# Trunk kernel, layer 0: indexer products over all 128 rows with stacks one pair ahead, shorter top-k rounds, packed rotation, later statistics

## The chip, the cores and the metric

The kernel runs on one core of one Trainium2 chip. The metric is the device time of one execution in microseconds (us), lower is better. All matrix products are float32, most of them as three products of rounded high and low parts.

## The reference, cut to what matters

A two-layer trunk over 1024 tokens of width 1024. Only layer 0's first mixer is touched. Cut down, it is:

```python
proj = xn @ w_in
q, k, v, u, iq, iw, ik = jnp.split(proj, AB_SPLITS, axis=-1)
q = rope_partial(rmsnorm(q, q_gain), pos)    # 4 heads of 128, the first 32 rows turned
k = rope_partial(rmsnorm(k, k_gain), pos)
iq = rope_partial(iq, pos)                   # 16 index heads of 64
ik = rope_partial(ik, pos)                   # one index key of 64
s = jnp.einsum('bqhd,bsd->bqhs', iqb, ik)    # per block of 128 queries
scores = jnp.einsum('bqhs,bqh->bqs', jax.nn.relu(s), iwb)
scores = jnp.where(causal, scores, -jnp.inf)
_, idx = lax.top_k(scores, 256)              # 256 keys per query
p = softmax(q . k[idx] * scale); a = p @ v[idx]
b = multiscale_pool(u, pool_w) * pool_scale  # windows 2, 4, 8, 16
h = h + jnp.concatenate([a, b]) @ w_out
```

## The kernel before, in words

Arrays are held transposed, features on the 128 partitions and tokens along the free axis. A float32 matrix is split into a rounded part (hi) and a rest (lo), and one product is three TensorE instructions (`mm3`, lines 321 to 323). A scheduler orders the instructions of each engine ahead of time by the order of the program and its dependencies; `issue_after` keeps one TensorE instruction behind another.

**Indexer** (`mixer0`, lines 652 to 697). Sixteen index heads are worked off in eight pairs, m = 0 to 7. `iq_gemm(m)` (line 594) projects a pair to a 128-row tile: 24 matmuls of 512 columns and 24 of 256. At the head of pass m the tile is turned by position (lines 655 to 658: a shuffle on DVE, a product on POOL, a product and a sum on DVE) and made into two stacks of 128 rows, one per head: the head's hi rows in its own 64 partitions, its lo rows in the other 64 (ACT line 661, DVE line 662). Then for the query blocks i = 2 to 7 and both heads, the scores against nk = 128(i+1) keys are summed in PSUM from two products per 512 columns:

```python
nc.tensor.matmul(p[:, c:c + n], stk[j][:, q0:q0 + P], ikh[:, c:c + n], start=True, stop=False)
last = nc.tensor.matmul(p[:, c:c + n], stk[j][own, q0:q0 + P], ikl[own, c:c + n], start=False, stop=True)
```

The first (line 672) takes all 128 rows, the second (line 673) the 64 hi rows. ACT applies the ReLU out of PSUM (line 679, two PSUM buffers, seven SBUF ones), DVE adds the weighted result to the block's scores `sc[i]` (line 689, 687 for the first head). After each such step two steps (three matmuls each) of `iq_gemm(m + 2)` are put in, which last for 8 of the 12 steps of a pass with m < 6, and from m = 1 on one step of the first key head's product every fourth time.

**Search** (`top_k`, lines 719 to 790). The 256th largest score of each query is found bit by bit, for the blocks 5, 7, 6 together and then for 4, 3, 2: two passes of 16 rounds each, 64 rounds in all. In a round DVE counts, for two of the three blocks, the keys not below a candidate (line 738), ACT counts the third by a sum of signs (line 749, blocks 5 and 4), and four small DVE instructions on 128x3 make the next candidate (lines 752, 753, 755, 756).

**Projections** (lines 792 to 895), beside the search: four pool groups `u`, the key heads `k1` to `k3` and four query heads `q`, 48 matmuls of 512 columns each, in the order of `PROJ` (line 207), then 192 matmuls for v. For k and q `head_stats` (line 639) copies the product, squares it (ACT line 642), sums the squares with eight tiny matmuls into the one PSUM bank of tag B (line 348), and DVE and POOL make the inverse root (lines 339, 340; for q also line 342, copied at line 862). `rope` (lines 809 to 816) turns the first 32 rows of each head in two halves: shuffle and sum on DVE (813, 816), two products on POOL (814, 815). k is then scaled by its root (line 869), q goes to memory (line 863). The rest of an item (`out`) runs one item later.

**Attention** (lines 901 to 990) makes the bias from the found bound, and the softmax and its products for all four heads, first for blocks 5, 7, 6 between the rounds of the second search. Loads and stores stand on SP's queue in order; the weights come two blocks ahead, their hi parts made by ACT (line 105), their lo parts by POOL or DVE (line 106).

Of the kernel before, what the change touches and what calls it, by code (L numbers as in the profile page):

```python
# [19 lines left out]
P = 128  # L20
# [27 lines left out]
def trunk_kernel(ctx: ExitStack, tc: tile.TileContext, io, dbg=None):  # L48
# [158 lines left out]
    PROJ = ("u3", "k1", "u2", "q0", "u1", "k2", "u0", "q1", "k3", "q2", "q3")  # L207
# [327 lines left out]
    def mixer0(right):  # L535
# [94 lines left out]
        def key_gemm(hd):  # L630
            w = W.next()
            t = heads[hd] = A(name="k"), []
            for half in range(2):
                p = G(name="pqk")
                yield from gemm_steps(p, w, xn, half)
                head_stats(t[0], t[1], p, half, V_AK, None)
            yield

        def head_stats(t, rss, p, half, gain, post):
# [3 lines left out]
            ss = B(name="ss")  # L643
            token_sums(ss, sq, HALF)
            rss.append(rstd_of(ss[:, :4], 4, 1.0 / P, post=post))
# [5 lines left out]
        side, turns = side_steps(), 0  # L651
        for m in range(8):
# [3 lines left out]
            nc.gpsimd.tensor_tensor(iq, iq, ciq[:, 256:], op=ALU.mult)  # L656
            nc.vector.tensor_tensor(sh, sh, siq[:, 256:], op=ALU.mult)
            nc.vector.tensor_tensor(iq, iq, sh, op=ALU.add)
            stk = [A((P, QI), F32R, "stk") for _ in range(2)]
            for j, (own, other) in enumerate(((lo64, hi64), (hi64, lo64))):  # L660
                nc.scalar.activation(stk[j][own], iq[own], AF.Copy)
                nc.vector.tensor_tensor(stk[j][other], iq[own], stk[j][own].bitcast(F32), op=ALU.subtract)
            ahead = iq_gemm(m + 2) if m < 6 else iter(())
            next(ahead, None)
            for i in range(2, 8):
                nk = (i + 1) * P
                for j, own in enumerate((lo64, hi64)):
# [29 lines left out]
            run(ahead)  # L697
        run(side)
# [8 lines left out]
        ACT_COUNTS = (5, 4)  # L707
# [12 lines left out]
        def top_k(bt):  # L720
            n = len(bt)

            def col(dt, name):
                return cpool.tile([P, n], dt, name=nm(name))

            cnt, cand, ncand, base, ge, need, sgn, off = (col(F32, nme) for nme in (
                "cnt", "cand", "ncand", "base", "ge", "need", "sgn", "off"))
            bits, low = col(U32, "bits"), col(U32, "low")
            by_act = {b for b in range(n) if bt[b] in ACT_COUNTS}
            for b in range(n):  # L730
                nc.gpsimd.memset(need[:, b:b + 1], 2.0 * TOPK - (bt[b] + 1) * P if b in by_act else float(TOPK))
# [9 lines left out]
            def search():  # L741

                nc.vector.memset(base, 0.0)
                nc.vector.memset(cand, 32768.0)
                nc.vector.memset(ncand, 0.5 - 32768.0)
# [49 lines left out]
        cqk, sqk = (pp.tile([32, T], F32, name=n) for n in ("cqk", "sqk"))  # L795
        nc.sync.dma_start(cqk, io["rope_q"][0])
        nc.sync.dma_start(sqk, io["rope_q"][1])
# [4 lines left out]
        rsq = keyp.tile([P, 8, 4], F32, name="rsq")  # L802
# [3 lines left out]
        def ptile(name):  # L806
            return pp.tile([P, T], F32, tag="t", bufs=3, name=nm(name))

        def rope(t):
            for half in range(2):  # L810
                sh = H("xt")[:32]
                th = t[:32, hs(half)]
# [5 lines left out]
        kT, v, wins = [], [], []  # L818

        def pool_in(g):  # L820
# [24 lines left out]
            return out  # L845

        def head_in(which, hd):
            if hd in heads and not which:
                t, rss = heads[hd]
            else:  # L850
                w = W.next()
# [845 lines left out]
```

## Time and profile before

| | us |
|---|---|
| median of 3 runs (lowest to highest) | 3076.42 (3075.61 to 3080.59) |
| the profiled execution, device time | 3071.26 |
| its span | 3069.1 |
| PE busy | 2890.0 (94%) |
| DVE busy | 1962.0 (64%) |
| ACT busy | 1249.3 (41%) |
| POOL busy | 868.6 (28%) |

The span is what the hardware profiler saw between the first and the last instruction of the core. PE is TensorE, DVE VectorE, ACT ScalarE, POOL GpSimd, SP the queue of loads and stores. PE's instructions are pipelined, and their ends are modelled: the distance from one start to the next says more than a duration. PEclk is the granted TensorE clock, 1.00 for 2.4 GHz and 0.50 for 1.2 GHz; a mean between them is a mix in time. The stretch that the change touches goes from 113.9 us (first score product) to 722.4 us (first output product); after it the program is as it was.

### The profile page before, as it was taken

The numbers are of one execution on the slowest core, as the hardware profiler recorded it, in microseconds if no ns is written. First come the engines' busy times: TensorE is split into PE (matmuls) and PEld (weight loads), VectorE is DVE, ScalarE is ACT, GpSimd is POOL, SyncE is SP. The second block draws the span as 40 slices with busy tenths as digits, with TensorE's granted clock in tenths as the row PEclk, the third lists the DMA queues.
The fourth block names the chain that finished last, engine by engine and source line by source line (L and its number), as shares of the span: only waits on it lengthen the run. The fifth ranks groups of instructions, "written<-read, shape, count | busy, mean of one in ns | idle before, by whom it ended". The sixth has DMA issues, their size and how long they took to land. (4 is left out here: it accounts for less than half of the span.)

```text
span 3069.1 us, 36440 instructions
## 1 busy us (share of the span) xinstructions
PE 2890.0 (94%) x13022; PEld 2279.7 (74%) x13022; DVE 1962.0 (64%) x3092; ACT 1249.3 (41%) x2058; POOL 868.6 (28%) x661
## 2 busy tenths in 40 slices
PE   7999888899999989999999997999999999999999
PEld 6665566678888868887778765777788878777877
DVE  8666799985345584445775865666633554566876
ACT  6444333565354443333333314333545443322432
POOL 5311344221132154443330101001101344455332
PEclk9998788999999999999999998999999999999999
DMA  6200011324443424334535745775463334555544
GB/s 233 69 21 21 21 50 40 110 67 149 163 157 132 129 86 123 124 119 148 173 123 175 251 138 178 254 244 181 146 204 124 138 113 127 166 185 196 168 135 143
DMA packets 169637, 423.75 MB, mean 138 GB/s; under 512 B 19376, under 2 KB 33840, under 8 KB 169456
## 3 DMA queue, kind: packets, MB, share of 16 engines
q1 hardware_dynamic: 169456, 421.43, 42.0%
q8 instruction: 103, 1.69, 0.2%
q14 instruction: 78, 0.64, 0.1%
HBM read 323.18 MB, written 98.17 MB: 137 GB/s over the span
## 5 line engine op out<-in xcount | busy, mean ns | idle before, releaser
L105 ACT ACTIVATE w<-raw 128x512 fp32r<-128x512 f32 (+4 forms) x497 | 382.7, 786 | 615.5 <-POOL raw L169 126.8
L106 DVE TENSOR_TENSOR w<-raw,w 128x512 fp32r<-128x512 f32 (+3 forms) x438 | 417.0, 968 | 218.6 <-ACT w L105 216.8
L106 POOL TENSOR_TENSOR w<-raw,w 128x1024 fp32r<-128x1024 f32 (+1 forms) x59 | 145.6, 2470 | 365.3 <-ACT w L105 364.3
L167 POOL TENSOR_TENSOR acc<-raw 128x512 f32<-128x512 f32 (+1 forms) x64 | 85.0, 1329 | 410.6 <-DMA raw<-in_w_down 188.8
L106 DVE TENSOR_TENSOR w<-acc,w 128x512 fp32r<-128x512 f32 (+1 forms) x64 | 77.4, 1210 | 145.0 <-ACT w L105 144.9
L321 PE MATMUL pa<-T,w 128*128 128x512 f32 x352 | 139.9, 397 | 12.5 <-DVE sq L1236 9.0
L322 PE MATMUL pa<-T,w 128*128 128x512 f32 x352 | 138.9, 395 | 0.2 <-DVE T L106 0.2
L323 PE MATMUL pa<-T,w 128*128 128x512 f32 x352 | 138.6, 394 | 0.0
L738 DVE TENSOR_SCALAR_CACHE_REDUCE junk<-key,cand 128x896 uint16<-128x896 uint16 (+3 forms) x128 | 116.3, 942 | 1.9
L135 ACT ACTIVATE w<-raw 128x1024 fp32r<-128x1024 f32 (+1 forms) x72 | 68.0, 950 | 119.4 <-PE pa L323 26.5
L105 ACT ACTIVATE w<-acc 128x512 fp32r<-128x512 f32 (+1 forms) x64 | 38.9, 609 | 159.6 <-POOL acc L167 151.8
L749 ACT ACTIVATE sq<-key,ncand 128x768 bf16<-128x768 uint16 (+1 forms) x64 | 56.3, 880 | 115.3 <-DVE cand L756 106.5
L322 PE MATMUL pr<-o,w 128*128 128x512 f32 x256 | 101.6, 397 | 0.0
L321 PE MATMUL pq<-hn,w 128*128 128x512 f32 x256 | 101.0, 395 | 0.0
L322 PE MATMUL pq<-hn,w 128*128 128x512 f32 x256 | 100.1, 391 | 0.0
L323 PE MATMUL pr<-o,w 128*128 128x512 f32 x256 | 99.9, 392 | 0.0
L323 PE MATMUL pq<-hn,w 128*128 128x512 f32 x256 | 99.7, 389 | 0.0
L689 DVE SCALAR_TENSOR_TENSOR sc<-relu,iw,sc 128x640 f32<-128x640 f32 (+3 forms) x60 | 73.0, 1220 | 41.1 <-ACT relu L679 40.4
L321 PE MATMUL pr<-o,w 128*128 128x512 f32 x256 | 98.1, 397 | 0.7 <-DVE ha L1119 0.5
L361 DVE TENSOR_TENSOR acc<-acc,sq 128x512 f32<-128x512 f32 (+1 forms) x105 | 86.9, 829 | 17.3 <-ACT sq L359 13.8
L169 POOL TENSOR_TENSOR raw<-acc,raw 128x512 f32<-128x512 f32 (+1 forms) x64 | 93.6, 1462 | 5.4 <-DVE w L106 1.2
L1401 DVE SCALAR_TENSOR_TENSOR y<-gd,vecs,y 128x512 f32<-128x512 f32 x120 | 89.2, 747 | 6.0 <-ACT y L1397 6.0
(477 smaller groups left out, 8565.2 us busy)
## 6 DMA issues: line engine op xcount, KB each, us to landing
raw<-in_w_gate SPq DMA_DIRECT2D x62, 512.0 KB, 3.8
w<-lo SPq DMA_DIRECT2D x56, 512.0 KB, 4.5
raw<-in_conv_in SPq DMA_DIRECT2D x48, 512.0 KB, 4.8
raw<-in_w_up SPq DMA_DIRECT2D x44, 512.0 KB, 4.7
hid<-xt SPq DMA_DIRECT2D x88, 256.0 KB, 4.1
lo<-w SPq DMA_DIRECT2D x40, 512.0 KB, 2.9
raw<-in_wq SPq DMA_DIRECT2D x32, 512.0 KB, 4.1
raw<-in_wo SPq DMA_DIRECT2D x32, 512.0 KB, 4.1
```

The source lines that it names most:

```text
L105: nc.scalar.activation(hi, src, AF.Copy)
L106: (lo_eng or nc.vector).tensor_tensor(lo, src, hi.bitcast(F32), op=ALU.subtract)
L135: nc.scalar.activation(hi, raw, AF.Copy)
L167: PS.tensor_tensor(s1, a2[:, near], a2[:, far], op=ALU.add)
L169: PS.tensor_tensor(a1[:, near], s1, a1[:, near], op=ALU.subtract)
L321: nc.tensor.matmul(out, lh, rh, start=first, stop=False, skip_group_check=more)
L322: nc.tensor.matmul(out, lh, rl, start=False, stop=False, skip_group_check=more)
L323: nc.tensor.matmul(out, ll, rh, start=False, stop=last, skip_group_check=more)
L361: nc.vector.tensor_tensor(acc[:, :n], acc[:, :n], d[:, :n], op=ALU.add)
L689: nc.vector.scalar_tensor_tensor(sc[i], r, iw[:, i, hd:hd + 1], sc[i], op0=ALU.mult, op1=ALU.add)
L738: nc.vector.tensor_scalar(junk[turn[0]][:, :(bt[b] + 1) * P], data, bound, None, op0=ALU.is_ge, op1=ALU.add, accum_out=one(cnt, b))
L1401: nc.vector.scalar_tensor_tensor(acc, x, col(s), acc, op0=ALU.mult, op1=ALU.add)
```

## The change

The second product of the indexer takes all 128 rows, so that lo times lo is added. The stacks come from a pool of their own with four buffers, and `stack()` makes those of pair m + 1 in pieces during pass m, one piece per block i. ACT counts block 7 (1024 keys) in place of 5 (768), and turns its sum of signs into a count by one more small instruction; a round has two small DVE instructions in place of four. The statistics of a head are issued one product later (`wait`, `tick`), the pool groups' rest four products later. The order of the items changes. The first 32 rows of the four heads are gathered by SBUF to SBUF transfers into one 128-row tile, turned there once for k and once for q, and sent back; the keys are scaled before. The cosine and sine tables are loaded four times, one copy per quarter. The factor of the q roots goes into line 339's constants, and the roots are written where they are used.

```diff
-    PROJ = ("u3", "k1", "u2", "q0", "u1", "k2", "u0", "q1", "k3", "q2", "q3")
+    PROJ = ("u3", "k1", "u2", "k2", "u1", "k3", "u0", "q0", "q1", "q2", "q3")
...
-    def rstd_of(ss, n, inv, post=None):
+    def rstd_of(ss, n, inv, post=1.0, rs=None):
-        ms, rs = tiny(n, name="ms"), tiny(n, name="rs")
-        nc.vector.tensor_scalar(ms, ss, inv, EPS, op0=ALU.mult, op1=ALU.add)
+        ms, rs = tiny(n, name="ms"), tiny(n, name="rs") if rs is None else rs
+        nc.vector.tensor_scalar(ms, ss, inv / post ** 2, EPS / post ** 2, op0=ALU.mult, op1=ALU.add)
         nc.gpsimd.tensor_tensor(rs, ms, neghalf[:, :n], op=ALU.pow)
-        if post is not None:
-            nc.vector.tensor_scalar_mul(rs, rs, post)
...
+        def stack():
             iq = iqs.pop(0)
+            stk = [ikp.tile([P, QI], F32R, tag="stk", bufs=4, name=nm("stk")) for _ in range(2)]
             sh = A((P, QI), name="iqsh")
             nc.vector.stream_shuffle(sh, iq, swap8)
             nc.gpsimd.tensor_tensor(iq, iq, ciq[:, 256:], op=ALU.mult)
+            yield
             nc.vector.tensor_tensor(sh, sh, siq[:, 256:], op=ALU.mult)
+            yield
             nc.vector.tensor_tensor(iq, iq, sh, op=ALU.add)
-            stk = [A((P, QI), F32R, "stk") for _ in range(2)]
             for j, (own, other) in enumerate(((lo64, hi64), (hi64, lo64))):
+                yield
                 nc.scalar.activation(stk[j][own], iq[own], AF.Copy)
                 nc.vector.tensor_tensor(stk[j][other], iq[own], stk[j][own].bitcast(F32), op=ALU.subtract)
+            stacks.append(stk)
...
         for m in range(8):
+            stk = stacks.pop(0)
             ahead = iq_gemm(m + 2) if m < 6 else iter(())
             next(ahead, None)
+            turned = stack() if m < 7 else iter(())
             for i in range(2, 8):
+                next(turned, None)
...
-                        last = nc.tensor.matmul(p[:, c:c + n], stk[j][own, q0:q0 + P], ikl[own, c:c + n], start=False, stop=True)
+                        last = nc.tensor.matmul(p[:, c:c + n], stk[j][:, q0:q0 + P], ikl[:, c:c + n], start=False, stop=True)
...
-        ACT_COUNTS = (5, 4)
+        ACT_COUNTS = (7, 4)
...
                         if b in by_act:
-                            nc.scalar.activation(signs[:, :(bt[b] + 1) * P], key[bt[b]], AF.Sign, bias=one(ncand, b), accum_out=one(cnt, b))
+                            nk = (bt[b] + 1) * P
+                            nc.scalar.activation(signs[:, :nk], key[bt[b]], AF.Sign, scale=-1.0, bias=one(cand, b), accum_out=one(cnt, b))
+                            nc.scalar.activation(one(cnt, b), one(cnt, b), AF.Copy, scale=-0.5, bias=nk / 2)
                         else:
                             count(b, key[bt[b]], one(cand, b))
-                    nc.vector.scalar_tensor_tensor(ge, cnt, 1.0, need, op0=ALU.mult, op1=ALU.is_ge)
-                    nc.vector.scalar_tensor_tensor(base, ge, float(1 << bit), base, op0=ALU.mult, op1=ALU.add)
-                    if bit:
-                        nc.vector.tensor_scalar(ncand, base, -1.0, 0.5 - (1 << (bit - 1)), op0=ALU.mult, op1=ALU.add)
-                        nc.vector.tensor_scalar(cand, base, float(1 << (bit - 1)), None, op0=ALU.add)
+                    step = float(1 << bit)
+                    nc.vector.tensor_scalar(ge, cnt, float(TOPK), step, op0=ALU.is_ge, op1=ALU.mult)
+                    nc.vector.scalar_tensor_tensor(cand if bit else base, ge, -step / 2, cand, op0=ALU.add, op1=ALU.add)
...
+        def tick():
+            for e in pending:
+                e[0] -= 1
+            for e in [e for e in pending if e[0] <= 0]:
+                pending.remove(e)
+                e[1]()
...
+            def norm_k(t, half, rs):
+                bc = B(name="bc")
+                broadcast(bc, rs, range(4))
+                nc.vector.tensor_tensor(t[:, hs(half)], t[:, hs(half)], bc, op=ALU.mult)
...
+                nc.sync.dma_start(packed[0][quarter(hd)], t[:32])
+                kT.append(t)
+                if hd == 3:
+                    rope(packed[0])
+                    for i in range(4):
+                        nc.sync.dma_start(kT[i][:32], packed[0][quarter(i)])
...
+            for half in range(2):
+                p = G(name="pqk")
+                gemm_tile(p, w, xn, half)
+                stats = head_tile(t, p, half, gain)
+                tick()
                 if which:
-                    for half in range(2):
-                        nc.vector.tensor_copy(rsq[:, 4 * half:4 * half + 4, hd], rss[half])
-                    nc.sync.dma_start(qd[:, :, hd], t.rearrange("p (i q) -> p i q", q=P))
+                    wait(1, lambda half=half, stats=stats: stats(rsq[:, 4 * half:4 * half + 4, hd], P ** -0.5))
+                else:
+                    wait(1, lambda half=half, stats=stats: stat_k(t, half, stats))
+            if which:
+                nc.sync.dma_start(packed[1][quarter(hd)], t[:32])
+                nc.sync.dma_start(qd[32:, :, hd], t[32:].rearrange("p (i q) -> p i q", q=P))
+                if hd == 3:
+                    rope(packed[1])
+                    for i in range(4):
+                        nc.sync.dma_start(qd[:32, :, i], packed[1][quarter(i)].rearrange("p (i q) -> p i q", q=P))
```

`head_tile` is the old `head_stats` with the sums and the root put into a function that is called later; `rope` is the old one on 128 rows.

## Rows read from the trace of the kernel before

**Rows 1.** The windows view; columns: stretch (us), length, busy us (instructions) of each engine, PEclk, DMA share, GB/s

```profile
113.90:277.90 164.00, 163.97 (x577) 100.96 (x577) 107.85 (x111) 74.90 (x104) 30.05 (x14) 0.93 0.06 19
277.90:335.00 57.10, 56.89 (x96) 26.68 (x96) 31.84 (x36) 22.68 (x31) 6.17 (x9) 0.50 0.04 13
335.00:591.80 256.80, 212.97 (x910) 168.97 (x910) 242.10 (x574) 101.62 (x181) 109.67 (x78) 0.90 0.17 57
335.00:643.80 308.80, 253.26 (x1111) 198.67 (x1111) 290.87 (x731) 136.50 (x249) 125.94 (x90) 0.89 0.18 59
643.80:722.40 78.60, 74.77 (x527) 63.94 (x526) 54.97 (x161) 53.52 (x124) 22.21 (x28) 0.98 0.36 118
```

**Rows 2.** The timeline of PE, 258.2 to 259.9 us; columns: start us, duration us, instruction

```profile
258.20 0.39 PE L672 MATMUL psc<-ikh,stk 128*128 128x512 f32 x1
258.52 0.50 PE L673 MATMUL psc<-ikl,stk 64*128 64x512 f32 x1
258.95 0.50 PE L321 MATMUL pib<-xn,w 128*128 128x512 f32 x1
259.28 0.39 PE L322 MATMUL pib<-xn,w 128*128 128x512 f32 x1
259.51 0.39 PE L323 MATMUL pib<-xn,w 128*128 128x512 f32 x1
```

**Rows 3.** The groups by line of DVE, 100 to 760 us: the score sums

```profile
L689 DVE SCALAR_TENSOR_TENSOR sc<-relu,iw,sc 128x640 f32<-128x640 f32 (+3 forms) x60 | 73.0, 1220 | 41.1 <-ACT relu L679 40.4
...
L689 DVE SCALAR_TENSOR_TENSOR sc<-xt,iw,sc 128x384 f32<-128x384 f32 (+1 forms) x30 | 28.2, 942 | 34.4 <-ACT xt L679 34.3
```

**Rows 4.** The timeline of DVE, one round of each batch

```profile
400.95 1.28 DVE L738 TENSOR_SCALAR_CACHE_REDUCE junk<-key,cand 128x1024 uint16<-128x1024 uint16 x1
...
402.15 1.14 DVE L738 TENSOR_SCALAR_CACHE_REDUCE junk<-key,cand 128x896 uint16<-128x896 uint16 x1
...
403.40 0.16 DVE L752 SCALAR_TENSOR_TENSOR ge<-cnt,need 128x3 f32<-128x3 f32 x1
...
404.07 1.28 DVE L738 TENSOR_SCALAR_CACHE_REDUCE junk<-key,cand 128x1024 uint16<-128x1024 uint16 x1
...
589.45 0.74 DVE L738 TENSOR_SCALAR_CACHE_REDUCE junk<-key,cand 128x512 uint16<-128x512 uint16 x1
...
591.51 0.75 DVE L738 TENSOR_SCALAR_CACHE_REDUCE junk<-key,cand 128x512 uint16<-128x512 uint16 x1
```

**Rows 5.** The instructions of line 749 on ACT

```profile
L749 ACT ACTIVATE sq<-key,ncand x64: 813/876/937, 341.2 to 640.7; 128x768 bf16<-128x768 uint16 x32, 128x640 bf16<-128x640 uint16 x32
L749 ACT ACTIVATION_READ_ACCUMULATOR sq<-key,ncand x64: 185/186/194, 342.0 to 641.4; 128x1 f32 x64
```

**Rows 6.** The groups by line of DVE, 100 to 760 us: the small instructions of a round

```profile
L755 DVE TENSOR_SCALAR ncand<-base 128x3 f32<-128x3 f32 x60 | 20.9, 348 | 1.6
...
L753 DVE SCALAR_TENSOR_TENSOR base<-ge,base 128x3 f32<-128x3 f32 x64 | 17.8, 277 | 1.7
...
L752 DVE SCALAR_TENSOR_TENSOR ge<-cnt,need 128x3 f32<-128x3 f32 x64 | 16.1, 251 | 4.0
...
L756 DVE TENSOR_SCALAR cand<-base 128x3 f32<-128x3 f32 x60 | 14.7, 244 | 0.0
```

**Rows 7.** Windows of one line each: 813 and 816 on DVE, 814 and 815 on POOL

```profile
310.00:643.80 333.80, 11.36 (x32) 0.86 0.17 55
...
310.00:643.80 333.80, 13.45 (x16) 0.86 0.17 55
...
310.00:643.80 333.80, 24.97 (x16) 0.86 0.17 55
...
310.00:643.80 333.80, 25.92 (x16) 0.86 0.17 55
```

**Rows 8.** The waits of PE, 335 to 720 us; columns: total us, times, longest us

```profile
PE ss L348 <- ACT sq L642: 13.2, 2, 9.6
```

**Rows 9.** The waits of SP's queue, 335 to 720 us

```profile
SPq L863 <- DVE qk L816: 24.4, 2, 23.5
```

More of the change, by code (lines that the diff above doesn't have):

```diff
@@ L628, in mixer0, with head_tile @@
         heads = {}
-        def key_gemm(hd):
-            w = W.next()
-            t = heads[hd] = A(name="k"), []
-            for half in range(2):
[L634 to L639, printed above, removed]
+        rsq = scp.tile([P, 8, 4], F32, name="rsq")
+        def head_tile(t, p, half, gain):
             nc.scalar.activation(t[:, hs(half)], p, AF.Copy, scale=vcol(gain))
@@ L642, in head_stats, with stats, key_gemm @@
             nc.scalar.activation(sq, p, AF.Square)
-            ss = B(name="ss")
-            token_sums(ss, sq, HALF)
-            rss.append(rstd_of(ss[:, :4], 4, 1.0 / P, post=post))
+            def stats(rs=None, post=1.0):
+                ss = B(name="ss")
+                token_sums(ss, sq, HALF)
+                return rstd_of(ss[:, :4], 4, 1.0 / P, post=post, rs=rs)
+            return stats
+        def key_gemm(hd):
+            w = W.next()
+            t, rss = heads[hd] = A(name="k"), []
+            behind = None
+            for half in range(2):
+                p = G(name="pqk")
+                for n, _ in enumerate(gemm_steps(p, w, xn, half)):
+                    if n == 3 and behind:
+                        rss.append(behind())
+                    yield
+                behind = head_tile(t, p, half, V_AK)
+            yield
+            yield
+            rss.append(behind())
         def side_steps():
@@ L649, in side_steps @@
                 yield from key_gemm(int(name[1]))
-        side, turns = side_steps(), 0
-        for m in range(8):
+        stacks = []
+        def stack():
             iq = iqs.pop(0)
+            stk = [ikp.tile([P, QI], F32R, tag="stk", bufs=4, name=nm("stk")) for _ in range(2)]
             sh = A((P, QI), name="iqsh")
@@ L697, in mixer0 @@
             run(ahead)
+            run(turned)
         run(side)
@@ L794, in mixer0 @@
         pp = pool(p2, "proj")
-        cqk, sqk = (pp.tile([32, T], F32, name=n) for n in ("cqk", "sqk"))
-        nc.sync.dma_start(cqk, io["rope_q"][0])
-        nc.sync.dma_start(sqk, io["rope_q"][1])
+        cqk, sqk = (pp.tile([P, T], F32, name=n) for n in ("cqk", "sqk"))
+        for hd in range(4):
+            nc.sync.dma_start(cqk[32 * hd:32 * hd + 32], io["rope_q"][0])
+            nc.sync.dma_start(sqk[32 * hd:32 * hd + 32], io["rope_q"][1])
         poolw = pp.tile([P, 4, P], F32, name="poolw")
@@ L806, in ptile, with quarter, rope @@
         def ptile(name):
-            return pp.tile([P, T], F32, tag="t", bufs=3, name=nm(name))
-        def rope(t):
+            return pp.tile([P, T], F32, tag="t", bufs=4, name=nm(name))
+        def quarter(hd):
+            return slice(32 * hd, 32 * hd + 32)
+        def rope(pk):
             for half in range(2):
-                sh = H("xt")[:32]
-                th = t[:32, hs(half)]
+                sh = H("xt")
+                th = pk[:, hs(half)]
                 nc.vector.stream_shuffle(sh, th, swap16)
@@ L818, in mixer0, with wait @@
         kT, v, wins = [], [], []
+        packed = [pp.tile([P, T], F32, name=nm("pack")) for _ in range(2)]
+        pending = []
+        def wait(n, fn):
+            pending.append([n, fn])
+        def tick():
[4 more added lines that the diff above has]
+                e[1]()
         def pool_in(g):
@@ L844, in out @@
                 nc.sync.dma_start(bd[g], u)
-            return out
+            wait(4, out)
         def head_in(which, hd):
+            gain = V_AQ if which else V_AK
+            done = []
+            def norm_k(t, half, rs):
+                bc = B(name="bc")
+                broadcast(bc, rs, range(4))
+                nc.vector.tensor_tensor(t[:, hs(half)], t[:, hs(half)], bc, op=ALU.mult)
+                done.append(half)
+                if len(done) < 2:
+                    return
+                nc.sync.dma_start(packed[0][quarter(hd)], t[:32])
[4 more added lines that the diff above has]
+                        nc.sync.dma_start(kT[i][:32], packed[0][quarter(i)])
+                        tap(f"k{i}", kT[i])
@@ L848, in head_in, with stat_k @@
+            def stat_k(t, half, stats):
+                rs = stats()
+                wait(2, lambda: norm_k(t, half, rs))
             if hd in heads and not which:
                 t, rss = heads[hd]
-            else:
-                w = W.next()
-                t, rss = ptile("qk") if which else A(name="k"), []
                 for half in range(2):
-                    p = G(name="pqk")
-                    gemm_tile(p, w, xn, half)
-                    head_stats(t, rss, p, half, V_AQ if which else V_AK, P ** -0.5 if which else None)
@@ L872, in head_in @@
-            return out
-        out = None
+                    norm_k(t, half, rss[half])
+                return
+            w = W.next()
+            t = ptile("qk") if which else A(name="k")
+            for half in range(2):
+                p = G(name="pqk")
+                gemm_tile(p, w, xn, half)
+                stats = head_tile(t, p, half, gain)
+                tick()
+                if which:
+                    wait(1, lambda half=half, stats=stats: stats(rsq[:, 4 * half:4 * half + 4, hd], P ** -0.5))
+                else:
+                    wait(1, lambda half=half, stats=stats: stat_k(t, half, stats))
```

41 lines of the change are left out of this document (15 added, 26 removed).

## The prediction, before the changed kernel was run

> **What bounds the kernel now.** I read the windows view first, because shares of the whole span mean nothing here: only 113.9 to 722.4 us are touched. From 113.9 to 335.0 us, the indexer, PE is busy all the time (163.97 of 164.00 and 56.89 of 57.10 us) and DVE two thirds or less [rows 1]: TensorE bounds it. In its last two passes (277.9 to 335.0 us), where only score products are left, the granted clock is 0.50, the lower level of 1.2 GHz, although PE does not rest. From 335.0 to 643.8 us, until the second search is done, it is the other way: DVE is busy 290.87 of 308.80 us and PE stands still for 55 us [rows 1]. So DVE bounds the search, and the projections beside it end at 591.8 us because they wait for DVE and ACT in between. The last 78.6 us of attention keep PE at 95% [rows 1]; they move as a whole if both search and projections end earlier.
>
> Then the timeline of PE shows why the indexer's products are dear. Two 512-column products on 128 rows follow one another at 0.23 us (259.28 to 259.51). From a 128-row product to a 64-row one it takes 0.32, from the 64-row one back 0.43, and the next product still 0.33 before the pace is 0.23 again [rows 2]. A pair so takes 0.75 us, and 0.10 of the follower, where two 128-row products would take 0.46.
>
> **Part 1, the indexer.** Before: 164.0 us for six passes (27.3 each) and 57.1 us for the last two, together 221.1 us.
> After, on PE at full clock: a head has 4224 columns in two products, so a pass has 2 x 2 x 4224/512 x 0.23 = 7.6 us; the projection two pairs ahead has 24 products of 512 and 24 of 256 columns, 24 x 0.23 + 24 x 0.115 = 8.3 us; the key head's 48 products are spread at 2.1 us a pass. Sum 18.0 us a pass.
> DVE needs 107.85/6 = 18.0 us a pass, measured [rows 1], which the change leaves: the turning moves within the pass, and nothing of it goes. So the two engines become equal, and DVE is late next. ACT is at 74.90/6 = 12.5 us. Making the stacks during the pass before is what lets DVE run on; at the head of a pass PE now finds its stacks ready.
> Two engines of equal load with two PSUM buffers between them lose something at hand-overs; no row prices that. It is between nothing and what PE would lose if its score products still fell to 1.2 GHz (15.2 us for 7.6; 25.6 us a pass). I take 20.5 us, nearer to the low end, since the long runs at 0.50 stood where 64-row products alternated. Pass 6 has no projection: DVE's 18.0 bounds it. Pass 7 has no turning either: twelve sums at 101.2/90 = 1.12 us [rows 3] are 13.5 us, PE at the lower clock needs 15.2; I take 15. Sum 6 x 20.5 + 18 + 15 = 156 us, a gain of **65 us**. Bounds: 7 x 18 + 13.5 = 139.5 us (gain 82), and 6 x 25.6 + 33 = 187 us (gain 34).
>
> **Part 2, the rounds.** A round of the first batch is 3.12 us (400.95 to 404.07), of which the four small instructions take 0.67; one of the second is 2.06 us (589.45 to 591.51) [rows 4]. Two dependent small ones at 0.2 each are 0.40, so 0.27 us go. In the first batch DVE counts 768 keys instead of 1024: 1.20 us for 1024 (to 402.15) is 0.15 per 128, so 0.9 in place of 1.2, of which I count 0.27. Gain 32 x 0.54 + 32 x 0.27 = 26 us.
> ACT's side: 0.81 us for 640 and 0.94 for 768 keys, so some 1.15 for 1024 (an estimate from these two), then 0.19 for reading the sum [rows 5], then the added 128x1 instruction, which the trace does not have. It costs at least nothing and at most the 0.81 of a whole count; it is nearest to the 0.19 of the read, so 0.2. That makes 1.54 us in the first batch, against some 2.1 of counting on DVE: covered. In the second, 1.2 against 2.06 - 0.67 = 1.39: covered by 0.2 only. At 0.81 it would stick out by 0.42 us, 13 us in 32 rounds.
>
> **Part 3, the rotation.** Shuffles and sums cost DVE 11.36 + 13.45 = 24.8 us, the products POOL 24.97 + 25.92 = 50.9 us [rows 7]. On 128 rows at once it is 4 halves in place of 16: DVE saves three quarters, 18.6, of which I count 17 for overlapped ends. The dropped copy and factor, sixteen small instructions at 0.16 us, give 2.5 more.
> The four small instructions of a round stand at 20.9 + 17.8 + 16.1 + 14.7 = 69.5 us for 248 [rows 6], while one alone is 0.16 [rows 4], 39.7 us: 30 us are spent being held up. By what, no row here says; I take it to be POOL's products beside them. POOL is busy 125.94 us there [rows 1]; the rotation's 38 us less are 30% of it, so 9 of the 30 us go (bounds 0 and 25).
> The transfers that come in (six more loads of tables, four out and four back for k, four into the packed tile and four out of it for q, beside the four stores of the other rows) have no path of their own to the end: the last, q's, comes before v's 192 products at 0.23, 44 us, which cover it. Without that cover it would cost two halves of turning, (24.8 + 50.9)/16 x 2 = 9.5 us, and its transfers.
>
> **Part 4, later statistics.** PE waited 13.2 us for the squares [rows 8]; one product later they are there. PE's projections must gain as much as the search, or they bound. Their products alone are (11 x 48 + 192) x 0.23 = 166 us of the 256.8 to 591.8 us [rows 1]: 91 us are to be had, so DVE's pace decides.
> DVE in sum: 26 + 17 + 2.5 + 9 = 55 us of 309. The B bank still has one buffer, whose reader on DVE stands between counts, so I count **50 us** (bounds 25 and 75).
>
> **Sum.** 65 + 50 = 115 us. The terms come from the profiled execution: 3071.26 - 115 = 2956; the median of the runs is 5.2 above it, so I predict 2961. After 722.4 us nothing changes.
>
> **Rivals.**
> *1. The rows don't matter, 3026 us.* If a 64-row product cost by its columns and the distance in rows 2 came from something else, say from writing to the same PSUM bank, widening gives nothing: only the 50 us are left. Against it: products that follow one another into one bank (the pib ones) keep 0.23. The Trainium skill has that rule, in "TensorE: Matmul & The Clock Gate", section "Why this matters for your kernels": a product with few rows takes the time of a 128-row one. By that rule the sum would be 3026; the trace, at 0.75 against 0.46 a pair, speaks against it. Chance 0.06.
> *2. The clock, 3048 us.* PE now has to wait for DVE. If the whole indexer ran at 1.2 GHz, PE would need twice its 7.6 x 8 + 8.3 x 6 + 11 = 122 us, 243 us instead of 221: the indexer would lose 22 of the search's 50, and 28 are left. For it: 0.50 in the last passes. Against: there every second product used half the rows; the six passes with projections on 128 rows among them had 0.93 [rows 1]. Chance 0.05.
> *3. More, below 2915 us.* Both engines of the indexer run without loss (82) and DVE's hold-ups vanish (75): 2919 or less. Chance 0.08.
> *4. Slower: SP's queue, about 3115 us.* Loads and stores issue in order, and each new transfer of the packed tiles waits on SP for DVE, with the weights' loads behind it. SP waited up to 23.5 us for one such store [rows 9]. If eight of them hold it so long, that is 188 us; two weights in stock cover 2 x 11 us, and 166 us less the 115 gained makes 51 longer, some 3115 to 3130. It decides from 17 us a transfer on (137 in all). Against it: the 23.5 us did not show as a wait of PE for weights. Chance 0.03.
> *5. Nothing moves*, since the engines' orders, which are made ahead, undo it: 3076. Chance 0.02.
>
> **How the numbers follow.** Forecast 0.76; with rivals 1 to 5 that is 1. The forecast's own range is 2919 to 3017, gains of 157 (82 + 75) down to 59 (34 + 25). The range is 2915 to 3017: rivals 1, 2, 4, 5 and most of 3 are left out, not quite 0.2 with the tails. Measurement of this kernel can tell 0.2%, about 6 us. Faster 0.95 (all but 4 and 5), same 0.02, slower 0.03.
>
> **What would show it.** Right: lines 672 and its follower 0.23 us apart; DVE above 85% in passes 0 to 5, which take about 20 us each; the first score product to the last in some 155 us; a first-batch round of 2.55 us, a second-batch one of 1.8; DVE's lines 813 and 816 at a quarter; no wait of PE for the squares; the first output product at about 607 us. Wrong: PEclk 0.50 through the indexer, ACT's count ending after DVE's in most rounds, waits of PE for weights with SP held by the packed tiles, or projections that end later than some 200 us after the indexer.

## The result, and the profile after

The changed kernel takes 2965.43 us (median of 4 runs, 2964.49 to 2970.61), the kernel before 3076.02 (four runs by then): a ratio of 0.9646, 95% interval 0.9624 to 0.9667. That is 109 us (102 to 116) less; 115 were predicted, and 2961.0 us. The profiled execution of after took 2966.34 us, its span 2964.6, against 3071.26 and 3069.1: 104.5 us of span.

The stages first, in the windows view (columns as in [rows 1]): the indexer, its passes 0 to 5 and 6 to 7, the projections up to the first attention product, attention up to the first output product.

```profile
118.70:271.30 152.60, 137.42 (x677) 111.80 (x678) 135.92 (x139) 95.10 (x133) 40.06 (x21) 0.96 0.08 25
118.70:240.00 121.30, 113.89 (x579) 94.39 (x579) 105.68 (x108) 73.33 (x104) 29.47 (x13) 0.99 0.07 22
240.00:271.30 31.30, 23.53 (x98) 17.42 (x99) 30.24 (x32) 21.78 (x31) 10.59 (x9) 0.84 0.11 35
271.30:498.10 226.80, 204.14 (x907) 165.39 (x907) 202.79 (x447) 121.59 (x241) 72.14 (x55) 0.94 0.25 75
498.10:620.30 122.20, 109.69 (x729) 90.33 (x728) 91.98 (x274) 86.72 (x197) 38.11 (x40) 0.97 0.33 106
```

Against [rows 1] the indexer lasts 152.6 us in place of 221.1, but it starts 4.8 us later (118.7 for 113.9), since the first stacks are now made ahead of the loop. PE is no longer busy all the time (137 of 152.6), DVE is busy 89%, and the last two passes run at 0.84 instead of 0.50, although PE rests in them. Projections take 227 us in place of 257, attention 122 in place of 131.

The timeline of PE inside the indexer (columns as in [rows 2]) has the two products of a pair at the common pace:

```profile
196.83 0.39 PE L695 MATMUL psc<-ikh,stk 128*128 128x512 f32 x1
197.06 0.39 PE L696 MATMUL psc<-ikl,stk 128*128 128x512 f32 x1
197.28 0.33 PE L695 MATMUL psc<-ikh,stk 128*128 128x384 f32 x1
```

0.23 us to the follower and 0.22 from there on: the 0.75 and 0.10 of [rows 2] are gone.

The timeline of DVE shows the shorter rounds: one quiet round of the first batch runs from 295.37 to 297.97, 2.60 us for the 3.12 of [rows 4], one of the second from 472.48 to 474.27, 1.79 for 2.06.

```profile
295.37 1.01 DVE L759 TENSOR_SCALAR_CACHE_REDUCE junk<-key,cand 128x768 uint16<-128x768 uint16 x1
...
297.57 0.17 DVE L774 TENSOR_SCALAR ge<-cnt 128x3 f32<-128x3 f32 x1
297.77 0.16 DVE L775 SCALAR_TENSOR_TENSOR cand<-ge,cand 128x3 f32<-128x3 f32 x1
297.97 1.01 DVE L759 TENSOR_SCALAR_CACHE_REDUCE junk<-key,cand 128x768 uint16<-128x768 uint16 x1
...
472.48 0.75 DVE L759 TENSOR_SCALAR_CACHE_REDUCE junk<-key,cand 128x512 uint16<-128x512 uint16 x1
...
474.27 0.75 DVE L759 TENSOR_SCALAR_CACHE_REDUCE junk<-key,cand 128x512 uint16<-128x512 uint16 x1
```

The groups by line of DVE hold the first surprise. There are 124 of the small instructions of a round where [rows 6] had 248 (four more, those of the last bits, stand in a row of their own), and they take 50.4 us; at 0.16 each it would be 19.8. The 30 us of hold-up are all still there:

```profile
L774 DVE TENSOR_SCALAR ge<-cnt 128x3 f32<-128x3 f32 x64 | 29.9, 467 | 11.9 <-ACT cnt L770 8.4
L775 DVE SCALAR_TENSOR_TENSOR cand<-ge,cand 128x3 f32<-128x3 f32 x60 | 20.5, 342 | 1.9 <-DVE ge L774 0.2
```

And the waits of PE from 271 to 625 us: the wait for the squares of [rows 8] is down from 13.2 to 1.7 us, and what is left are mostly waits for DVE, for small instructions and for one wide product (line 891).

```profile
PE bc L351 <- DVE ge L774: 8.2, 2, 5.2
PE ss L346 <- DVE ms L339: 6.0, 2, 5.9
...
PE bc L351 <- DVE k L891: 3.9, 1, 3.9
...
PE ss L346 <- ACT sq L634: 1.7, 1, 1.7
```

### The profile page after: what moved, and what is told of

Same layout as the page of the kernel before. It is cut to its first block, busy times and chain, and to the rows that moved or that the text cites. A ratio compares the mean times of both kernels' runs of the same rounds, so it can differ in the third digit from the quotient of the medians.

```text
span 2964.6 us, 36342 instructions
## 1 busy us (share of the span) xinstructions
PE 2788.1 (94%) x13022; PEld 2257.0 (76%) x13022; DVE 1905.7 (64%) x2912; ACT 1264.8 (43%) x2122; POOL 837.8 (28%) x631
## 5 line engine op out<-in xcount | busy, mean ns | idle before, releaser
L759 DVE TENSOR_SCALAR_CACHE_REDUCE junk<-key,cand 128x896 uint16<-128x896 uint16 (+3 forms) x128 | 107.9, 877 | 2.1
L769 ACT ACTIVATE sq<-key,cand 128x1024 bf16<-128x1024 uint16 (+1 forms) x64 | 63.2, 988 | 75.0 <-DVE cand L775 63.7
L321 PEld LDWEIGHTS pa<-T,w 128*128 128x128 f32 x352 | 67.4, 192 | 32.2 <-issue 12.8
```

What stands on the lines that cost most here:

```text
L321: nc.tensor.matmul(out, lh, rh, start=first, stop=False, skip_group_check=more)
L759: nc.vector.tensor_scalar(junk[turn[0]][:, :(bt[b] + 1) * P], data, bound, None, op0=ALU.is_ge, op1=ALU.add, accum_out=one(cnt, b))
L769: nc.scalar.activation(signs[:, :nk], key[bt[b]], AF.Sign, scale=-1.0, bias=one(cand, b), accum_out=one(cnt, b))
```

## The experiments

Ratios are to the kernel before in runs on the same chip; the gain is (1 - ratio) x 3076 us. The four times are those of the profiled run: start of the last score product, of the first attention product, of the first output product, and the span. They come from one execution each: behind the first output product, where the programs are the same, these executions differ by up to 14 us (2337.9 us in e7_split, 2352.2 in e9_allvec), so a few us between two spans mean nothing.

| kernel | ratio (95%) | gain, us | last score | attention | output | span |
|---|---|---|---|---|---|---|
| before | 1 | 0 | 333.1 | 591.9 | 722.5 | 3069.1 |
| the change | 0.9646 (0.9624 to 0.9667) | 109 | 270.3 | 498.3 | 620.3 | 2964.6 |
| e1_wide | 0.9786 (0.9771 to 0.9801) | 66 | 266.9 | 526.7 | 660.3 | 3007.2 |
| e2_index | 0.9798 (0.9783 to 0.9812) | 62 | 268.9 | 530.7 | 661.3 | 3006.7 |
| e3_rounds | 0.9939 (0.9918 to 0.9959) | 19 | 334.0 | 579.6 | 702.8 | 3042.6 |
| e4_proj | 0.9960 (0.9946 to 0.9973) | 12 | 331.4 | 571.6 | 709.9 | 3056.6 |
| e5_group | 0.9902 (0.9883 to 0.9921) | 30 | 298.3 | 557.1 | 686.9 | 3034.7 |
| e6_turn | 0.9643 (0.9626 to 0.9659) | 110 | 263.2 | 489.5 | 613.4 | 2958.1 |
| e7_split | 0.9620 (0.9601 to 0.9638) | 117 | 263.7 | 478.0 | 606.6 | 2944.5 |
| e8_inplace | 0.9664 (0.9645 to 0.9683) | 103 | 267.9 | 496.0 | 618.0 | 2958.7 |
| e9_allvec | 0.9588 (0.9568 to 0.9609) | 127 | 261.6 | 475.6 | 603.9 | 2956.1 |
| e10_oldrounds | 0.9725 (0.9703 to 0.9747) | 85 | 269.6 | 507.7 | 644.9 | 2988.2 |
| e11_oldproj | 0.9722 (0.9702 to 0.9743) | 86 | 269.8 | 519.0 | 644.5 | 2986.7 |
| e12_values | 0.9588 (0.9574 to 0.9602) | 127 | 260.2 | 473.0 | 601.3 | 2949.2 |

### Widening alone: e1_wide

```diff
-last = nc.tensor.matmul(..., stk[j][own, q0:q0 + P], ikl[own, c:c + n], ...)
+last = nc.tensor.matmul(..., stk[j][:, q0:q0 + P], ikl[:, c:c + n], ...)
```

> The kernel before, with the second score product over all 128 rows and nothing else; stacks are still made at the head of the pass that uses them. Theory (changing between 128-row and 64-row products costs time): the pair of products goes from 0.75 to 0.46 us, PE falls under DVE's 18 us a pass, but each pass begins with the wait for its stacks, some 3 to 5 us; passes of 21 to 23 us instead of 27.3, the last two together 38 to 42 instead of 57.1, so 35 to 50 us of the 64 are gained and the kernel takes 3026 to 3041. The granted clock of the last two passes rises to 0.8 or more. Rival 1 of the prediction (rows don't matter): 0 us, 3076. Rival (the stacks made ahead are the gain): under 15 us.

Measured: 66 us, the whole of the indexer's gain and more than I expected. Its last score product starts at 266.9 us, 3.4 us earlier than in the changed kernel, its first 4.7 us earlier (114.0 for 118.7). The wait for the stacks at the head of a pass, for which I had allowed 3 to 5 us a pass, is small: in all passes together PE waits 2.1 us for them.

### The indexer whole: e2_index

The edit is that of the diff: the second product, stack() one pair ahead, four buffers.

> The kernel before, with the indexer's part of the change whole: second product over 128 rows, stacks one pair ahead in four buffers of their own. Theory: the whole 64 us of the indexer, and nothing behind it, since the search is as before: 3010 to 3016. Rival (what the indexer wins is partly lost again behind it, because the later work waits for something that the indexer does not move, such as weights): 3025 or more.

Measured: 62 us, as the theory had it: what the indexer wins is passed on. But the stacks made ahead bring nothing. The groups by line of DVE from 110 to 275 us say why; first with the widening alone (e1_wide), then with the stacks ahead (after):

```profile
L689 DVE SCALAR_TENSOR_TENSOR sc<-relu,iw,sc 128x640 f32<-128x640 f32 (+3 forms) x60 | 75.2, 1277 | 4.6 <-ACT relu L679 3.4
L689 DVE SCALAR_TENSOR_TENSOR sc<-xt,iw,sc 128x384 f32<-128x384 f32 (+1 forms) x30 | 28.1, 945 | 7.2 <-ACT xt L679 6.7
...
L657 DVE TENSOR_TENSOR iqsh<-iqsh,siq 128x768 f32<-128x768 f32 x7 | 8.3, 1184 | 0.0
```

```profile
L712 DVE SCALAR_TENSOR_TENSOR sc<-relu,iw,sc 128x640 f32<-128x640 f32 (+3 forms) x60 | 73.9, 1249 | 10.1 <-ACT relu L702 8.8
L712 DVE SCALAR_TENSOR_TENSOR sc<-xt,iw,sc 128x384 f32<-128x384 f32 (+1 forms) x30 | 20.1, 682 | 2.2 <-ACT xt L702 1.3
L671 DVE TENSOR_TENSOR iqsh<-iqsh,siq 128x768 f32<-128x768 f32 x7 | 16.4, 2342 | 0.2
```

The small sums lose 8 us (28.1 to 20.1), and the product of the turning gains 8 (8.3 to 16.4). DVE is as busy as before (135.9 us against 137.4 in windows of 153 us), and it sets the length.

### The rounds alone, and the projections alone: e3_rounds, e4_proj

Both are parts of the diff: e3 has search() and ACT_COUNTS, e4 the order PROJ, the packed tiles and the later statistics.

> The kernel before, with the shorter rounds alone (two small instructions in place of four, the count of 1024 keys on ACT in place of 640). The prediction's step: 32 rounds x 0.54 and 32 x 0.27, all of it on the path, 26 us: 3050. Theory now (the first attention step waits for the projections on PE, not for the search, so a shorter search counts only where it hands DVE back to the projections and to the second batch): 8 to 16 us, 3060 to 3068; the first round of the first batch is 2.6 us all the same. Rival (rounds off the path entirely): 0, 3076.

> The kernel before, with the projections' part of the change alone (new order, turning in packed tiles, later statistics), indexer and rounds as before. The prediction's step: 17 + 2.5 + 9 us less DVE work, 28 us: 3048. Theory now (the projections on PE set the start of attention; each of their waits that goes is time won, whoever's instructions cause it): 20 to 30 us, 3046 to 3056, with the wait for the squares (13.2 us) down to 2. If the three parts add up, e2, e3 and e4 together gain what the whole change gains, 105 to 111 us. Rival (rounds and projections relieve the same engine, so either alone gives most of the 38): e3 and e4 together over 50 us.

Measured: 19 and 12 us. e3 gains 13.2 of them before attention begins and 7.4 within it (by the table, from the last score product on). e4 brings attention forward by 18.6 us, and attention then lasts 7.7 longer (138.3 for 130.6). I had expected less of the rounds and more of e4: a wait of 8.9 us for the squares remains in it. e2, e3 and e4 sum to 93 us, the change has 109.

### Taking one part back: e10_oldrounds, e11_oldproj

> The changed kernel with the rounds as before. Alone on the kernel before, the shorter rounds gave 19 us and the projections' part 12; with the indexer's 62 to 66 that is 93 to 97, but the whole change gives 109. Theory (search and projections wait for one another: with the projections alone earlier, attention begins earlier but then stands for the second batch's search, and the other way round, so each is worth more beside the other): 25 to 33 us slower than the changed kernel, a ratio to the kernel before of 0.973 to 0.976. Rival (the parts are independent, the missing 12 us are the chips' spread): 19 us slower, 0.971 or less.

> The changed kernel with the projections' part as before (order, turning by head, early statistics). Theory as for the kernel with the old rounds: 20 to 28 us slower than the changed kernel, a ratio to the kernel before of 0.971 to 0.974. Rival (independent parts): 12 us slower, 0.969 or less.

Measured: the rounds are worth 24 us in the changed kernel (109 - 85), the projections 23 (109 - 86), against 19 and 12 alone. That is near the theory for both, but 24 and 23 are differences of two measured ratios, good to some 9 us: the interval of e10 begins at 0.9703 and so holds the rival's 0.971 too, that of e11 begins at 0.9702, just above its rival's 0.969. By the table the old rounds cost 10 us before attention and 15 within it, the old projections 21 and 4. Where the 15 are is in the windows view, the second twelve microseconds of attention, first after, then e10_oldrounds:

```profile
510.20:522.20 12.00, 10.30 (x54) 6.77 (x53) 11.46 (x37) 10.72 (x24) 5.97 (x5) 1.00 0.49 154
```

```profile
519.60:531.60 12.00, 5.95 (x18) 3.13 (x17) 11.69 (x36) 9.52 (x17) 4.14 (x3) 0.93 0.45 149
```

DVE is busy over 95% in both, for it does the rest of the second search beside the softmax; with the longer rounds PE gets 6 us of work there and with the shorter ones 10. So projections that end earlier meet a DVE that is still searching, and it takes the shorter rounds to use them. I show this for one stretch, and it does not hold of all 15 us: a gap as large, 11.93 us of PE's work from 534.20 to 546.20 us in after against 7.35 from 543.60 to 555.60 in e10_oldrounds, has DVE busy only 8.70 of the 12 us there. What cost the time in that one is open.

### What a change of rows costs: e5_group

```diff
 for c in range(0, nk, 512):
     n = min(512, nk - c)
     nc.tensor.matmul(p[:, c:c + n], stk[j][:, q0:q0 + P], ikh[:, c:c + n], ...)
+for c in range(0, nk, 512):
+    n = min(512, nk - c)
     last = nc.tensor.matmul(p[:, c:c + n], stk[j][own, q0:q0 + P], ikl[own, c:c + n], ...)
```

> The kernel before, the 64-row second product kept, but a head of 640 to 1024 keys runs its two 128-row products first and its two 64-row products after them: 12 changes of row count each way in a pass in place of 20, the same products. Theory (the change between 128 and 64 rows costs, 0.09 + 0.20 + 0.10 us for there and back): 64 round trips of 0.39 us less, 25 us: 3045 to 3052. Rival A (a 64-row product is dear by itself, or the rows don't matter): 0, 3070 to 3076. Rival B (the gain of the widening is the clock that alternating rows keeps low): the last two passes stay at 0.50 and the gain stands in none of them, under 10 us.

Measured: 30 us (24 to 36), all of it ahead of the last score product, which comes 34.8 us earlier. The same 64-row products, put next to each other, are not dear; the timeline of PE (x2 is two instructions in one row):

```profile
221.91 0.51 PE L672 MATMUL psc<-ikh,stk 128*128 128x512 f32 x2
222.36 0.61 PE L675 MATMUL psc<-ikl,stk 64*128 64x512 f32 x2
222.90 0.38 PE L321 MATMUL pia<-xn,w 128*128 128x256 f32 x1
```

Two products of 128 rows take 0.45 us and two of 64 rows 0.54 where two pairs took 1.50. Rival A falls. Of rival B one half stands: towards the end the granted clock stays at the low level, in the windows view of e5_group (two stretches) and then of e1_wide (the last two passes begin at 253.2 us in the one, at 236.5 in the other):

```profile
114.90:256.00 141.10, 140.52 (x587) 91.87 (x587) 109.01 (x112) 76.90 (x108) 31.11 (x15) 0.98 0.07 23
256.00:298.80 42.80, 40.64 (x83) 20.64 (x83) 29.87 (x34) 19.10 (x26) 6.94 (x7) 0.52 0.04 13
```

```profile
241.00:267.30 26.30, 20.50 (x82) 15.23 (x82) 25.27 (x31) 16.73 (x22) 6.50 (x5) 0.81 0.07 21
```

Its other half falls: by the starts of the passes the first six take 138.3 us for 164.7, the last two 45.1 for 54.5, so some 9 us of the gain stand where the clock is low. In the first six the clock rises as well (0.98 for the 0.93 of [rows 1]), and no run separates that from the changes of row count.

With 128 rows throughout, the end of the indexer gets most of the clock back (0.81 for 0.50). That this is part of the 66 us is not shown: the last two passes of e1_wide take 30.4 us, and twice the prediction's 15.2 us for PE at the lower clock would be as much.

### Who holds DVE up: e6_turn, e7_split, e9_allvec, e12_values

Before these I laid the timelines of DVE and POOL of the changed kernel side by side. One stretch of POOL and then of DVE, where the last instructions of the first batch's search meet the packed turning:

```profile
402.83 1.29 POOL L837 TENSOR_TENSOR pack<-pack,cqk 128x512 f32<-128x512 f32 x1 [12.80 <-DVE xt L836]
404.09 1.29 POOL L838 TENSOR_TENSOR xt<-xt,sqk 128x512 f32<-128x512 f32 x1
405.34 1.30 POOL L837 TENSOR_TENSOR pack<-pack,cqk 128x512 f32<-128x512 f32 x1
406.59 1.27 POOL L838 TENSOR_TENSOR xt<-xt,sqk 128x512 f32<-128x512 f32 x1
407.81 2.35 POOL L106 TENSOR_TENSOR w<-raw,w 128x1024 fp32r<-128x1024 f32 x1
```

```profile
403.30 0.85 DVE L774 TENSOR_SCALAR ge<-cnt 128x3 f32<-128x3 f32 x1
404.19 1.21 DVE L775 SCALAR_TENSOR_TENSOR base<-ge,cand 128x3 f32<-128x3 f32 x1
405.43 1.22 DVE L803 TENSOR_TENSOR cand<-base,sgn 128x3 f32<-128x3 f32 x1
406.69 1.19 DVE L804 TENSOR_TENSOR low<-cand,off 128x3 uint32<-128x3 f32 x1
407.91 2.26 DVE L805 TENSOR_TENSOR bits<-bits,low 128x3 uint32<-128x3 uint32 x1
```

Five instructions on three columns end within 0.03 us of the end of the POOL instruction that they meet (404.15 to 404.12, 405.40 to 405.38, and so on). The Trainium skill says so in "SBUF — State Buffer", section "Who interferes with whom": a pair of ports that VectorE and GpSimd share is locked for a whole instruction, and the other waits; these rows agree, 2.26 us for work of 0.16.

Of all 140 three-column instructions of the search with a float32 result, 25 took over 0.25 us, together 32 us beyond 0.16 each. By the POOL instruction that overlaps most, 20 of the 32 stand beside the subtraction that makes the low half of a weight (line 106), 5.5 beside the packed turning, 5.4 beside window sums. In the kernel before the same count gives 29, of which 12.4 beside the weights and 9.4 beside the turning.

```diff
 # e6_turn: in stack()
-nc.gpsimd.tensor_tensor(iq, iq, ciq[:, 256:], op=ALU.mult)
+nc.vector.tensor_tensor(iq, iq, ciq[:, 256:], op=ALU.mult)
 # e7_split: in add_proj
-W.add(io["w0"][...], eng=PL)
+W.add(io["w0"][...], eng=None if name in PROJ else PL)
```

> The changed kernel, with the turning's product on POOL (768 columns) moved to DVE. In the changed kernel DVE's own product of the turning takes 2.34 us where it took 1.18 with the widening alone, and with the widening alone the sums of 384 and 512 keys took 0.95 where they take 0.68: the same 8 us of hold-up in another place. Theory (whatever DVE instruction meets the POOL product waits for it): DVE gains 8 us of hold-up and pays 7 products of about 1.2 us, so the time stays within 4 us of the changed kernel, and DVE's product falls to 1.2. Rival (the hold-up is of DVE's own making, e.g. its operand arriving late): DVE's product stays at 2.3 and the kernel is 6 to 9 us slower.

> The changed kernel, with the subtraction that makes the low half of the eleven projection weights on DVE instead of POOL. Theory (the small instructions of a round are held up by POOL's 1024-column subtractions: 20 of their 32 us beyond 0.16 stand beside these): the hold-up falls from some 31 to 12 us, DVE pays 11 x 1.1 = 12 us, so the search ends 4 to 10 us earlier and the kernel takes 2955 to 2962. Rival 1 (the prediction's: the hold-up goes with POOL's busy time, of which this takes a third): hold-up falls by 10, DVE pays 12, 0 to +4. Rival 2 (the hold-up is only where such time shows, and something else takes it): small instructions at 0.16, no gain, 2965 to 2980.

Measured, e6: no difference (0.9643 against 0.9646), though in its own trace the first score product to the last takes 146.7 us for the changed kernel's 151.6, a gain too small for these intervals. DVE's old product fell to 1.25 us, but the one moved to DVE takes its place, beside the weight subtraction, in the groups by line of e6_turn:

```profile
L712 DVE SCALAR_TENSOR_TENSOR sc<-relu,iw,sc 128x640 f32<-128x640 f32 (+3 forms) x60 | 63.7, 1079 | 8.4 <-ACT relu L702 7.7
...
L669 DVE TENSOR_TENSOR iq<-iq,ciq 128x768 f32<-128x768 f32 x7 | 16.3, 2333 | 0.2
...
L671 DVE TENSOR_TENSOR iqsh<-iqsh,siq 128x768 f32<-128x768 f32 x7 | 8.8, 1252 | 0.0
```

So I had named the wrong POOL instruction for the 2.34 us: there too it was a weight's subtraction, and the POOL product held up the large sums behind it, which fell by 10 us.

e7: 8 us better than the changed kernel, though the two intervals just overlap (0.9601 to 0.9638 and 0.9624 to 0.9667). The hold-up, counted as above, falls from 32 to 18 us (12 were expected; what is left stands beside the value weights, the window sums and the turning), and attention begins 20.3 us earlier but then lasts 6.6 us longer (128.6 for 122.0). The small instructions of e7_split:

```profile
L774 DVE TENSOR_SCALAR ge<-cnt 128x3 f32<-128x3 f32 x64 | 21.4, 334 | 6.5 <-ACT cnt L770 2.8 <-DVE junk L759 0.5
L775 DVE SCALAR_TENSOR_TENSOR cand<-ge,cand 128x3 f32<-128x3 f32 x60 | 16.9, 281 | 1.6
```

DVE's wait for ACT's count fell with it, from 8.4 to 2.8 us, and the eleven subtractions cost DVE some 13 us (1.22 each). So DVE's own account is about even, and what part of the gain is the hold-up's and what part ACT's count is not shown.

e9_allvec joins both edits and takes the other weights of the indexer off POOL as well; e12_values adds the value weights' two:

> The changed kernel with no wide POOL instruction beside the scores and fewer beside the search: the turning's product and the low halves of all twenty of these weights on DVE. Theory (a DVE instruction that meets a wide two-operand POOL instruction waits until it ends, whichever the two are): with both POOL groups gone, all hold-up in the indexer goes: the sums of 640 to 1024 keys fall from 1.25 to about 1.05 us, those of 384 and 512 stay at 0.68, every product of the turning takes 0.95 to 1.25; that is some 20 us of hold-up against 17 us of new work in the indexer, and the 9 us of the projections as with the projection weights alone: 8 to 14 us faster than the changed kernel, ratio 0.960 to 0.962. Rival (DVE is overloaded, the hold-up was covered): indexer longer by 10 or more, ratio 0.965 or higher.

> The changed kernel with the turning's product and the low halves of all these weights on DVE, and two subtractions more: the value weights' two that POOL had. Theory (a small DVE instruction that meets a wide POOL instruction waits for its end): of the 18 us of hold-up left in the rounds up to 4 us go, for 2 x 1.2 us of new work on DVE: within 4 us of the kernel before this step, ratio 0.957 to 0.962; this also tells whether the 18 us that the step before won on the changed kernel stand on another chip. Rival (what gained was POOL's free time, not DVE's hold-up): no less hold-up, ratio 0.962 or more.

Measured: 0.9588 twice, on two chips: 18 us better than the changed kernel, with intervals that don't touch it. That is more than the 8 to 14 expected. In e9_allvec the hold-up is gone from the indexer altogether:

```profile
L712 DVE SCALAR_TENSOR_TENSOR sc<-relu,iw,sc 128x640 f32<-128x640 f32 (+3 forms) x60 | 64.0, 1085 | 13.5 <-ACT relu L702 13.3
...
L671 DVE TENSOR_TENSOR iqsh<-iqsh,siq 128x768 f32<-128x768 f32 x7 | 6.7, 956 | 0.0
```

Every DVE instruction there keeps one duration per shape, and the extra work (16 us on lines 106 and 669) costs no more than the waits did. From first to last score product it is 146.5 us for the changed kernel's 151.6, from there to attention 214.0 for 228.0. But e6_turn alone has 146.7 us in the first of these, and e7_split alone 147.3 and 214.3: the two edits do not add up. From the first score product to the first output product it is 488.8 us in e9, 490.2 in e7 and 501.6 in the changed kernel, the hold-up of the search is 18 us in e9 as in e7, and the intervals of these two overlap; what e9 has over e7 is not shown to be real. Of e12's own step nothing shows in the ratio, though the hold-up falls to 16 us. Both e9_allvec and e12_values are faster than the changed kernel and than the one before.

### The stacks in place: e8_inplace

The changed kernel with `run(stack())` at the head of each pass and the old buffers.

> The changed kernel, with the stacks made at the head of the pass that uses them, as before, the second product over 128 rows. Theory (DVE bounds the indexer, so when the stacks are made does not matter; the first stacks made one pair ahead even start the scores 4 us later): 0 to 5 us faster, 2960 to 2966. The prediction's step (making them in the pass before lets DVE run on): passes longer by 3 to 5 us, the kernel slower by 20 or more.

Measured: 0.9664 against 0.9646, 5 us apart with overlapping intervals. The first score product starts 4 us earlier, the last 2.4 us earlier; the prediction's 20 us are excluded.

## Why the prediction was right, and where it was not

**The indexer** was right in mechanism and size. 156 us were predicted, 152.6 measured; passes 0 to 5 take 20.2 us on average (121.3 / 6) for 20.5, the last two 31.3 for 33. That the 20.5 came so close is in part luck: it was a choice between 18.0 and 25.6, and no row had the price of the hand-overs. DVE is busy 105.68 of 121.3 us, 87%. Rival 1 falls: e1 shows the widening to give everything, and e5 that it is the change between 128 and 64 rows that costs. The Trainium skill names such a cost in "TensorEngine Tiling (Array Packing)", section "Key Properties" (a change of tiling mode drains the engine), without a figure; that these 64-row products are such a change, no run here shows. The price here is the 0.39 us of [rows 2]: e5's 64 round trips at 0.39 would be 25 us of its 30, and the better clock of the first six passes has a part in the 30. Wrong was one sentence of it: "Making the stacks during the pass before is what lets DVE run on". DVE was not held by where the stacks stood (e2, e8). And the later start, 4.8 us, was not counted.

**The rounds**: 2.55 and 1.8 predicted, 2.60 and 1.79 measured, and ACT's count of 1024 keys (1.15 us) and its added instruction (0.20) cost what was estimated, although the two rows that the 1.15 came from give 1.20 on a straight line. They are covered in 51 of the 64 rounds; in the other 13 DVE waits 8.4 us in all, where it did not wait before. Of the 26 us in sum, 19 come alone and 24 beside the rest; of the 28 for the projections' part 12 and 23. What failed was to count each microsecond that DVE saves as one that the kernel wins, from whichever part it comes.

**Hold-ups**, "the rotation's 38 us less are 30% of it, so 9 of the 30 us go": this step failed. POOL's products were rightly suspected, but the amount does not follow POOL's busy time. That fell by the 30% (125.94 us in the kernel before, 88.1 in the changed one, until the second search is done). The hold-up stayed at 30 us, on half as many small instructions: the share beside the turning fell, from 9.4 to 5.5 us, and the weights' subtractions took over, from 12 to 20 us. e4_proj, with the old rounds, has the same by the same count: 2.8 us beside the turning, 20.0 beside the weights, 34 in all. DVE's saving on shuffles and sums is as said (4 of each, 5.5 us for 24.8).

**The stage in sum**: 50 us predicted, 39 measured in the profiled runs (30.8 before attention, 8.6 in it). By the terms of the sum, the 9 us of hold-up that did not go are most of the difference; no run takes them apart from the rest. The sentence "91 us are to be had, so DVE's pace decides" was badly sized: PE is busy 204 of 226.8 us, since the 166 us of products leave out the small products for statistics, broadcasts and windows (26 us), and the stretches at a lower clock. What could be had was 44 us (256.8 - 213.0), and 30 were. Neither engine seems to decide alone: the stage gains 39 us in the changed kernel, 20.6 in e3 and 10.9 in e4, and e10 and e11 point the same way, within their noise.

**The end**: the first output product was predicted at 607 us and stands at 620.3: 4.8 from the later start of the indexer, 11 from the stage, less 2.6 from the indexer (first to last score product 151.6 us for 219.2, a gain of 67.6 in place of 65). After it the kernels differ by 2.3 us. **Rival 2** (clock) falls: 0.96 in the indexer. **Rivals 3 and 5** fall by the time itself. **Rival 4** (SP's queue) falls: SP waits for the packed tiles (35.9 us in four waits on line 895, the longest 13.8), and no wait of PE for a projection weight above 0.2 us follows.

## What to carry to other kernels

Look for products that alternate between row counts before looking at their columns: make them equal, or put equal ones together. A price list of instructions taken where they stand undisturbed shows who is held up: sum what exceeds it, and find what runs on POOL at that moment; moving that work to DVE can cost DVE time and still win. A part that shortens one of two engines that feed a stage can look cheap alone, so measure it beside the other too.

## What the runs showed of the hardware that I had not expected

- Not every DVE instruction is held up by POOL. The counts of the search (one wide operand, with a sum) stay at their quiet length in all 128 cases of the changed kernel (602 to 1146 ns, and 1.14 us is the quiet time for 896 keys), 12 of which begin while a wide POOL product or subtraction runs, and the shuffles of the indexer at 1.01 to 1.05 us, while products, sums and three-column instructions last up to 2.2 us longer than when undisturbed.
- TensorE's clock went to the lower level while PE was busy 56.89 of 57.10 us [rows 1], with every second product on 64 rows, and stayed near the upper one (0.81 to 0.84) with 128-row products and PE resting a fifth to a quarter of the time. e5, with 64-row products grouped, kept 0.52. Why, no run here shows.
